# Stick-breaking attention: the scan's products less 1, times differences of neighbouring rows of v, in place of differences of the products times v

## The chip, the core and the metric

The kernel runs on one core of a Trainium2 chip, in float32 throughout. The metric is the device time of one execution in microseconds (us). Work goes to five instruction queues that each run in order: PE (the matrix engine), DVE (vector), ACT (scalar), POOL (GpSimd) and SP, which only issues transfers (DMAs). The order on each engine is fixed when the program is built: a scheduler places the instructions by its own estimates, and the chip doesn't reorder them. An instruction that waits therefore holds up all that is queued behind it on its engine.

## What is computed

One layer of a hybrid decoder for 1024 positions of width 1024: a projection into three groups (short convolution, attention with 8 heads of 64, a spatial gating unit), an output projection, a squared-ReLU MLP and a gated embedding, each with a residual. The change is in the attention. For query t, with z its products with the keys:

```python
log_beta = jax.nn.log_sigmoid(z)
log_rem = jnp.where(causal, jax.nn.log_sigmoid(-z), 0.0)
suffix = lax.cumsum(log_rem, axis=3, reverse=True) - log_rem
weights = jnp.where(causal, jnp.exp(log_beta + suffix), 0.0)
o = jnp.einsum('bhqk,bkhd->bqhd', weights, vj)
```

With r[s] the product of sigmoid(-z) over all causal positions from s on (and 1 past the last), the weight of position s is r[s+1] - r[s]. So o is the sum over s of (r[s+1] - r[s]) v[s]. Summed by parts, the same o is the sum of (r[s] - 1)(v[s-1] - v[s]), with v[-1] = 0: the differences can be taken along the keys of v once per head, in place of along the keys of r for every query.

## The kernel before

Matrix products keep near float32 precision by splitting an operand into a rounded part "hi" (ACT writes it) and the remainder "lo" (mostly DVE, sometimes POOL): the helper `split`, L131 to L139. A product is three matmuls (L161 to L163).

The attention runs in four passes, one for a pair of heads each. `project(pr)` (L345) makes q, k and v of a pair: for each of eight tiles t of 128 positions it runs 24 matmuls of 384 columns into a bank `qkv_ps`, of which there are two. It then reads the bank: squares on ACT (L376), sums on DVE (L379), the power -1/2 on POOL (`rs`, L170), the scaled `qk` on DVE (L384), and v as V hi on ACT and V lo on DVE (L137, L138). Only then is the bank free, so tile t+2 can't start on PE before this chain of tile t has ended. `turn_qk` (L395) then turns q and k and writes QS, KH and KL.

`attend(pr)` (L423) has two generators. `stick` makes, for two query tiles, the products z on PE, the sigmoid on ACT into `rem` (L452), the running product from the right on DVE (`scan`, L457), and then `wt`, the differences of neighbouring columns of `rem` (L464): on DVE for t in (3, 5, 7), on POOL for t in (0, 1, 2, 4, 6), with a memset of the last column on POOL (L463). `gather` turns `wt` on PE (L486) into a bank `w_tr`, splits it into wT_hi and wT_lo (L489), and multiplies by V into `av` (L504). `rem` has 3 buffers and `wt` 4.

`weave` (L269) interleaves the attention of a pair with the projection of the next pair (for the last pair with the convolution) by counted units, so on PE both stand in one queue. The first projection runs without an attention beside it. The results of a head are added by a transfer that POOL issues (`y_both`, L515) and stored by SP (`y_dram`, L435). Between the steps, POOL and ACT issue transfers that add up blocks of later weights in DRAM (`w_sums`, `u_sums`, L305, L308, L322). They are issued behind the last `wt` of POOL and the last sigmoid of ACT (L293, `last_pool`, `last_act`).

SP issues the weights of the coming projections into 7 stage buffers (L67), and the stores, all in one queue. After the attention follow the output projection, the two MLP products and the gate (L814), which take some two thirds of the time.

Of the kernel before, what the change touches and what calls it, by code (L numbers as in the profile page):

```python
# [7 lines left out]
F32 = mybir.dt.float32  # L8
# [6 lines left out]
P = 128  # L15
# [8 lines left out]
STAGES = 7  # L24
WBUFS = 20
SLOTS = 56
LATE = {"w": 22, "raw": 4, "sum": 6, "tmp": 12, "R": 2}
KC = 8
WARM = 8
# [4 lines left out]
def hybrid_block(ctx: ExitStack, tc: tile.TileContext, a: dict):  # L34
# [93 lines left out]

    last_hi, last_power = [None], [None]

    def split(src, hi, lo, scale=None, low=nc.vector):  # L131

        if scale is None:
            last_hi[0] = nc.scalar.copy(hi, src)  # L134
            low.tensor_tensor(out=lo, in0=src, in1=hi, op=ALU.subtract)  # L135
        else:
            nc.scalar.activation(hi, src, AF.Copy, scale=scale)  # L137
            nc.vector.scalar_tensor_tensor(out=lo, in0=src, scalar=scale, in1=hi,  # L138
                                           op0=ALU.mult, op1=ALU.subtract)  # L139
# [199 lines left out]
    last_pool, last_act = [None], [None]  # L339
    summed = []  # L340
    heads = {}
    y_kept = []
# [2 lines left out]
    def project(pr):  # L345
# [11 lines left out]
        for t in range(KT):  # L357
# [24 lines left out]
            if t % 2 == 0:  # L382
# [2 lines left out]
                out=qk[:, t % 2].rearrange("p (h d) -> p h d", d=HD),  # L385
                in0=ps[:, :256].rearrange("p (h d) -> p h d", d=HD),
                in1=rs.unsqueeze(2).broadcast_to([P, 4, HD]), op=ALU.mult)
            if t % 2 == 0:
                V[t // 2] = slot("V", F32R, (P, 2, 2, 2, HD))
            v = V[t // 2][:, t % 2]  # L390
            split(ps[:, 256:].rearrange("p (h d) -> p h d", d=HD), v[:, :, 0], v[:, :, 1], scale=r1[t])
            if t % 2 == 1:
                later(72, lambda t=t, qk=qk: turn_qk(heads[pr], t, qk))

    def turn_qk(head, t, qk):  # L395

# [26 lines left out]
    def attend(pr):  # L423
# [13 lines left out]
        def stick(hh, g):  # L437
            weights[hh, g] = []
            for t in (2 * g, 2 * g + 1):
                W = (t + 1) * P  # L440
                th, ts = block(t)
                rem = at.tile([P, T], F32, tag="rem", name=name("rem"), bufs=3)
                wt = at.tile([P, T], F32, tag="wt", name=name("wt"), bufs=4)
                for kh in reversed(range(th + 1)):
                    n = min(HT, W - kh * HT)
                    ks = slice(kh * HT, kh * HT + n)
                    z = bank(ps_z, "z")[:, :n]
                    nc.tensor.matmul(z, QS[hh][th][:, ts], KH[hh][kh][:, :n],
                                     start=True, stop=False)
                    nc.tensor.matmul(z, QS[hh][th][:, ts], KL[hh][kh][:, :n],  # L450
                                     start=False, stop=True)
                    last_act[0] = nc.scalar.activation(rem[:, ks], z, AF.Sigmoid,  # L452
                                                       scale=-HD ** -0.5)


                back = rem[:, :W][:, ::-1]
                nc.vector.tensor_tensor_scan(out=back, data0=back,  # L457
                                             data1=after[:, T - W:][:, ::-1], initial=1.0,
                                             op0=ALU.mult, op1=ALU.max)


                on_vector = t in (3, 5, 7)
                nc.gpsimd.memset(wt[:, W - 1:W], 0.0)  # L463
                done = (nc.vector if on_vector else nc.gpsimd).tensor_tensor(  # L464
                    out=wt[:, :W - 1], in0=rem[:, 1:W], in1=rem[:, :W - 1], op=ALU.subtract)
                if not on_vector:
                    last_pool[0] = done
                weights[hh, g].append(wt)
                yield 2 * (t + 1) + 8

        def gather(hh, g):
# [5 lines left out]
            def turn(j):  # L477
# [8 lines left out]
                        nc.tensor.transpose(tr[:, n:n + P], wts[i][:, kb * P:(kb + 1) * P], ident)  # L486
# [40 lines left out]
    def attention():  # L527
# [6 lines left out]
        for i, (pr, *step) in enumerate(steps):  # L534
            if i + 1 < len(steps):
                nxt, *ahead = steps[i + 1]
                if nxt not in parts:
                    parts[nxt] = attend(nxt)
                yield from parts[nxt][0](*ahead)
            block_sums(i, (last_pool[0], last_act[0]))  # L540
            if pr == 3:
                up_sums(last_pool[0], last_act[0])
            yield from parts[pr][1](*step)
            if i % 2 == 1:
                parts[pr][2]()
            if i % 8 == 7:
                yield None
# [10 lines left out]
    def gating():  # L558
# [35 lines left out]
        for t in range(KT):  # L594
# [6 lines left out]
                root(th)  # L601
                yield 1
            if t % 4 == 0:
                vp = [at.tile([P, 4, 4 * HD], F32R, tag="rem", name=name("vn"), bufs=3)
                      for _ in range(2)]
                vus = []
            if t % 2 == 0:
                vus.append(at.tile([P, 2, HT], F32, tag="wt", name=name("vu"), bufs=4))
# [74 lines left out]
    for n in range(KT):  # L683
# [1 line left out]
        st = stage(a["w_vu"][n])  # L685
        vu_parts.append(pair("vu"))
        split(st, *vu_parts[n])
        pp = at.tile([P, T], F32, tag="wt", name=name("pp"), bufs=4)
# [368 lines left out]


    g_sums = dram.tile([4, 4, P, HT], F32, name="g_sums")
    pace = const.tile([P, 2], F32, name="pace")  # L1060
    def gate_sums(i, behind):

        if not 0 <= i < 16:
# [281 lines left out]
```

## Time and profile before

| | us |
|---|---|
| three runs | 1208.08, 1208.18, 1209.59 |
| median of the runs | 1208.18 |
| the profiled execution, first to last instruction (span) | 1205.0 |
| attention and its projections, about | 75 to 410 of the span |

The profile gives no time of its own for the profiled execution beside the span. The median run is 3.2 us longer than the span, which lies before the first and after the last instruction. In the tables that follow, "busy" is the time in which an engine executed, and the name behind an arrow is what ended the idle time before an instruction. Busy times of matmuls that follow each other overlap. A row of a timeline begins with the start in us from the span's start and the duration in us.

### The profile page before, as it was taken

The numbers are of one execution on the slowest core, as the hardware profiler recorded it, in microseconds if no ns is written. First come the engines' busy times: TensorE is split into PE (matmuls) and PEld (weight loads), VectorE is DVE, ScalarE is ACT, GpSimd is POOL, SyncE is SP. The second block draws the span as 40 slices with busy tenths as digits, with TensorE's granted clock in tenths as the row PEclk, the third lists the DMA queues.
The fourth block names the chain that finished last, engine by engine and source line by source line (L and its number), as shares of the span: only waits on it lengthen the run. The fifth ranks groups of instructions, "written<-read, shape, count | busy, mean of one in ns | idle before, by whom it ended". The sixth has DMA issues, their size and how long they took to land.

```text
span 1205.0 us, 17538 instructions
## 1 busy us (share of the span) xinstructions
PE 1181.0 (98%) x5788; PEld 1007.1 (84%) x5788; DVE 885.7 (73%) x1310; ACT 595.5 (49%) x1148; POOL 400.5 (33%) x472
## 2 busy tenths in 40 slices
PE   9999899998999999999999999999999999999997
PEld 7899899898888888888888888888888888888886
DVE  7846898989896667868877777787664657753697
ACT  7735565565643466733334333356543444456642
POOL 3324355464352222045354453421023301013412
PEclk9999999999999999999999999999999999999999
DMA  9602359999673776679998989777889975644857
GB/s 311 233 18 90 130 172 262 253 194 167 140 146 95 196 263 204 204 207 261 265 240 249 264 238 260 221 257 277 300 267 295 290 249 175 231 146 119 181 155 209
DMA packets 127963, 254.03 MB, mean 211 GB/s; under 512 B 14496, under 2 KB 22432, under 8 KB 127168
## 3 DMA queue, kind: packets, MB, share of 16 engines
q1 hardware_dynamic: 94992, 168.08, 41.4%
q0 software_dynamic: 27664, 57.05, 25.2%
q10 hardware_dynamic: 5216, 27.79, 6.4%
q8 instruction: 45, 0.74, 0.3%
q14 instruction: 46, 0.38, 0.1%
HBM read 192.30 MB, written 92.80 MB: 237 GB/s over the span
## 4 chain that ended last, share of the span: by engine, by line
PE 88%; DVE 8%; ACT 1%; issue 1%; DMA 1%; POOL 1%; SPq 0%; DVEq 0%; ACTq 0%; POOLq 0%
PE f_ps L814 25%; PE d_ps L814 25%; PE g_ps L814 6%; DVE rem L457 3%; PE qkv_ps L161 3%; PE qkv_ps L162 2%; PE qkv_ps L163 2%; PE o_ps L161 2%; PE o_ps L163 2%; PE o_ps L162 2%; PE av L504 2%; PE cv_ps L163 2%; PE cv_ps L161 2%; PE cv_ps L162 2%; PE w_tr L486 1%; PE vu_ps L162 1%
## 5 line engine op out<-in xcount | busy, mean ns | idle before, releaser
L135 DVE TENSOR_TENSOR w_lo<-raw,w_hi 128x512 fp32r<-128x512 f32 x280 | 243.1, 872 | 85.0 <-ACT w_hi L134 83.1
L134 ACT CAST w_hi<-raw 128x512 fp32r<-128x512 f32 x280 | 172.5, 620 | 240.5 <-PE d_ps L814 115.4
L814 PE MATMUL f_ps<-hn_hi,w_hi 128*128 128x512 f32 x448 | 175.2, 392 | 0.0
L814 PE MATMUL f_ps<-hn_lo,w_hi 128*128 128x512 f32 x448 | 174.9, 390 | 0.0
L814 PE MATMUL d_ps<-f_hi,w_hi 128*128 128x512 f32 x448 | 174.8, 390 | 0.0
L814 PE MATMUL f_ps<-hn_hi,w_lo 128*128 128x512 f32 x448 | 174.6, 391 | 0.0
L814 PE MATMUL d_ps<-f_hi,w_lo 128*128 128x512 f32 x448 | 174.3, 389 | 0.0
L814 PE MATMUL d_ps<-f_lo,w_hi 128*128 128x512 f32 x448 | 174.3, 389 | 0.0
L457 DVE TENSOR_TENSOR_SCAN rem<-rem,after 128x128 f32<-128x128 f32 (+3 forms) x64 | 90.9, 1431 | 13.3 <-ACT rem L452 13.3
L814 PEld LDWEIGHTS f_ps<-hn_lo,w_hi 128*128 128x128 f32 x448 | 84.5, 189 | 17.9 <-issue 0.2
L814 PEld LDWEIGHTS f_ps<-hn_hi,w_hi 128*128 128x128 f32 x448 | 84.5, 189 | 17.8 <-issue 0.2
L814 PEld LDWEIGHTS f_ps<-hn_hi,w_lo 128*128 128x128 f32 x448 | 84.5, 189 | 17.6
L814 PEld LDWEIGHTS d_ps<-f_hi,w_hi 128*128 128x128 f32 x448 | 84.1, 188 | 17.7 <-issue 0.2
L814 PEld LDWEIGHTS d_ps<-f_hi,w_lo 128*128 128x128 f32 x448 | 84.1, 188 | 17.6
L814 PEld LDWEIGHTS d_ps<-f_lo,w_hi 128*128 128x128 f32 x448 | 84.1, 188 | 17.5 <-issue 0.2
L161 PE MATMUL qkv_ps<-whi,xn_hi 128*128 128x384 f32 x256 | 88.8, 347 | 0.9 <-DVE V L138 0.8
L162 PE MATMUL qkv_ps<-wlo,xn_hi 128*128 128x384 f32 x256 | 86.6, 338 | 0.0
L163 PE MATMUL qkv_ps<-whi,xn_lo 128*128 128x384 f32 x256 | 86.3, 337 | 0.0
L135 DVE TENSOR_TENSOR f_lo<-raw,f_hi 128x512 fp32r<-128x512 f32 x112 | 78.2, 728 | 8.5 <-ACT f_hi L134 8.2
L134 ACT CAST f_hi<-raw 128x512 fp32r<-128x512 f32 x112 | 67.1, 620 | 25.6 <-DMA raw<-f_dram 21.6
L800 POOL TENSOR_TENSOR S<-S,sq 128x512 f32<-128x512 f32 x19 | 25.6, 1347 | 160.1 <-ACT sq L876 160.1
L452 ACT ACTIVATE rem<-z 128x128 f32<-128x128 f32 (+3 forms) x96 | 46.7, 500 | 24.3 <-PE z L450 21.6
(250 smaller groups left out, 2618.9 us busy)
## 6 DMA issues: line engine op xcount, KB each, us to landing
raw<-in_w_ff SPq DMA_DIRECT2D x148, 256.0 KB, 4.2
raw<-f_dram SPq DMA_DIRECT2D x112, 256.0 KB, 5.1
raw<-w_sums SPq DMA_DIRECT2D x64, 256.0 KB, 4.1
f_dram<-f SPq DMA_DIRECT2D x48, 256.0 KB, 3.9
f_dram<-t SPq DMA_DIRECT2D x48, 256.0 KB, 4.0
w_sums<-in_w_ff POOLq DMA_DIRECT2D x8, 1024.0 KB, 12.1
w_sums<-w_sums POOLq DMA_DIRECT2D x8, 1024.0 KB, 15.3
raw<-in_w_out SPq DMA_DIRECT2D x28, 256.0 KB, 3.5
```

The lines of the kernel that those rows point to most:

```text
L134: last_hi[0] = nc.scalar.copy(hi, src)
L135: low.tensor_tensor(out=lo, in0=src, in1=hi, op=ALU.subtract)
L161: nc.tensor.matmul(ps, lh, rh, start=first and i == 0, stop=False)
L162: nc.tensor.matmul(ps, lh, rl, start=False, stop=False)
L163: done = nc.tensor.matmul(ps, ll, rh, start=False, stop=last and i == len(terms) - 1)
L452: last_act[0] = nc.scalar.activation(rem[:, ks], z, AF.Sigmoid, scale=-HD ** -0.5)
L457: nc.vector.tensor_tensor_scan(out=back, data0=back, data1=after[:, T - W:][:, ::-1], initial=1.0, op0=ALU.mult, op1=ALU.max)
L486: nc.tensor.transpose(tr[:, n:n + P], wts[i][:, kb * P:(kb + 1) * P], ident)
L504: nc.tensor.matmul(av[:, first * P:], lhs, part[:, o:o + m], start=kb == 0 and part is hi, stop=kb == 2 * g + 1 and part is lo)
L800: return eng.tensor_tensor(out=out, in0=x, in1=y, op=ALU.add)
L814: done = nc.tensor.matmul(bank, l, r, start=first and k == 0 and i == 0, stop=k == len(b) - 1 and i == 2, skip_group_check=True)
```

## The change

1. `stick` no longer makes `wt`: the 64 differences (24 on DVE, 40 on POOL) and the 64 memsets on POOL go. `gather` turns `rem` itself. `rem` now has 6 buffers and serves also the gating unit's and the embedding's tiles that had been in `wt`.
2. The 80 splits of `w_tr` subtract 1 on the way: hi is an ACT activation with a bias of -1, lo is a three-operand instruction of DVE, (w_tr - 1) - hi.
3. v leaves the bank with one ACT instruction a tile into `v_raw`, which holds four tiles; the 32 V lo of DVE go.
4. After four tiles, `v_steps` makes the differences: SP moves `v_raw` down by one row (a transfer from rows 0 to 126 to rows 1 to 127 of `v_step`, one that brings three single rows from row 127, and, for the second half, one single row from the half before; for the first half a memset of one row on POOL), POOL subtracts `v_raw` (one instruction of 128x512), and each half of `v_step` is split: hi by a cast on ACT, lo on POOL. This happens twice for each pair of heads, eight times in all.
5. The transfers that add up weights are now issued behind a small copy on POOL (`pace`, 128x2) from the newest `rem`, 32 in all, since no `wt` is there to be issued behind.

```diff
+REMS = 6
...
-    def split(src, hi, lo, scale=None, low=nc.vector):
-
-        if scale is None:
+    def split(src, hi, lo, scale=None, low=nc.vector, offset=None):
+
+        if offset is not None:
+            nc.scalar.activation(hi, src, AF.Copy, bias=offset)
+            nc.vector.scalar_tensor_tensor(out=lo, in0=src, scalar=offset, in1=hi,
+                                           op0=ALU.add, op1=ALU.subtract)
+        elif scale is None:
...
-            if t % 2 == 0:
-                V[t // 2] = slot("V", F32R, (P, 2, 2, 2, HD))
-            v = V[t // 2][:, t % 2]
-            split(ps[:, 256:].rearrange("p (h d) -> p h d", d=HD), v[:, :, 0], v[:, :, 1], scale=r1[t])
+            if t % 4 == 0:
+                raw_before = raw if t else None
+                raw = at.tile([P, 4, P], F32, tag="v_raw", name=name("v_raw"), bufs=2)
+            nc.scalar.activation(raw[:, t % 4], ps[:, 256:], AF.Copy, scale=r1[t])
             if t % 2 == 1:
                 later(72, lambda t=t, qk=qk: turn_qk(heads[pr], t, qk))
+            if t % 4 == 3:
+                later(24, lambda th=th, v=raw, b=raw_before: v_steps(V, th, v, b))
+
+    def v_steps(V, th, raw, before):
+
+        step = slot("v_step", shape=(P, 4, P))
+        nc.sync.dma_start(step[1:], raw[:P - 1])
+        nc.sync.dma_start(step[:1, 1:], raw[P - 1:, :3])
+        if before is None:
+            nc.gpsimd.memset(step[:1, 0], 0.0)
+        else:
+            nc.sync.dma_start(step[:1, 0], before[P - 1:, 3])
+        nc.gpsimd.tensor_tensor(out=step, in0=step, in1=raw, op=ALU.subtract)
+        for j in range(2):
+            v = V[2 * th + j] = slot("V", F32R, (P, 2, 2, 2, HD))
+            split(step[:, 2 * j:2 * j + 2].rearrange("p t (h d) -> p t h d", d=HD),
+                  v[:, :, :, 0], v[:, :, :, 1], low=nc.gpsimd)
+        return 0
...
-                on_vector = t in (3, 5, 7)
-                nc.gpsimd.memset(wt[:, W - 1:W], 0.0)
-                done = (nc.vector if on_vector else nc.gpsimd).tensor_tensor(
-                    out=wt[:, :W - 1], in0=rem[:, 1:W], in1=rem[:, :W - 1], op=ALU.subtract)
-                if not on_vector:
-                    last_pool[0] = done
-                weights[hh, g].append(wt)
+                last_rem[0] = rem
+                weights[hh, g].append(rem)
...
-                split(tr[:, :n], hi[:, :n], lo[:, :n])
+                split(tr[:, :n], hi[:, :n], lo[:, :n], offset=-1.0)
...
+            last_pool[0] = nc.gpsimd.tensor_copy(pace, last_rem[0][:, :2])
             block_sums(i, (last_pool[0], last_act[0]))
```

The scheduler places the new instructions among the old. Two places matter below.

On POOL, at the end of the first projection, these rows stood before. `rs_1207`, `rs_1244`, `rs_1289` and `rs_1326` are the powers of the tiles 4, 5, 6 and 7, and `rs_1512` that of tile 0 of the second projection; a power is followed by DVE's `qk`, which frees a bank.

```order
L170 TENSOR_TENSOR rs_1207<-ss_1205,mhalf 128x4
L170 TENSOR_TENSOR rs_1244<-ss_1242,mhalf 128x4
L170 TENSOR_TENSOR rs_1289<-ss_1287,mhalf 128x4
L464 TENSOR_TENSOR wt_1348<-rem_1347 128x127
L464 TENSOR_TENSOR wt_1421<-rem_1420 128x255
L135 TENSOR_TENSOR wlo_1371<-stage_1368,whi_1370 128x384
```

At the same place the changed program has these rows. Here `rs_1214`, `rs_1250` and `rs_1294` are the powers of the tiles 4, 5 and 6.

```order
L175 TENSOR_TENSOR rs_1214<-ss_1212,mhalf 128x4
L409 MEMSET v_step_1198 1x128
L412 TENSOR_TENSOR v_step_1198<-v_step_1198,v_raw_993 128x512
L175 TENSOR_TENSOR rs_1250<-ss_1248,mhalf 128x4
L140 TENSOR_TENSOR V_1203<-v_step_1198,V_1203 128x4x64
L140 TENSOR_TENSOR V_1206<-v_step_1198,V_1206 128x4x64
L175 TENSOR_TENSOR rs_1294<-ss_1292,mhalf 128x4
```

Between the powers of tiles 4 and 5 now stands the subtraction that waits for SP's transfer of the first half of v, and two lo of V between those of tiles 5 and 6.

The second half of the same pair is met a little later, at the start of the second projection, where `rs_1508` and `rs_1594` are the powers of its tiles 0 and 1. Again POOL, changed program:

```order
L175 TENSOR_TENSOR rs_1508<-ss_1506,mhalf 128x4
L412 TENSOR_TENSOR v_step_1349<-v_step_1349,v_raw_1218 128x512
L175 TENSOR_TENSOR rs_1594<-ss_1592,mhalf 128x4
L368 MEMSET KL_1414 64x512
L368 MEMSET KL_1416 64x512
L140 TENSOR_TENSOR V_1354<-v_step_1349,V_1354 128x4x64
```

The subtraction again stands directly ahead of a power; before, nothing that waits for a transfer stood there.

On SP the transfers of that second half come after the weights of a coming projection (`stage`) and ahead of the stores of `y_both`:

```order
L68 DMA stage_3003<-in_w_qkv 128x384
L406 DMA v_step_1349<-v_raw_1218 127x512
L407 DMA v_step_1349<-v_raw_1218 1x16x24
L411 DMA v_step_1349<-v_raw_993 1x16x8
L459 DMA y_dram<-y_both_1481 64x512
```

The program carries the single rows as 16 pieces of 24 and of 8 numbers and a store as 64 rows; the big transfer it carries as 127 rows of 512 numbers.

More of the change, by code (lines that the diff above doesn't have):

```diff
@@ L337, in up_sums @@
                            lambda of: w_block("w_ff1", of, i // 4), nc.scalar)
-    last_pool, last_act = [None], [None]
+    last_pool, last_act, last_rem = [None], [None], [None]
+    pace = const.tile([P, 2], F32, name="pace")
     summed = []
@@ L441, in stick @@
                 th, ts = block(t)
-                rem = at.tile([P, T], F32, tag="rem", name=name("rem"), bufs=3)
-                wt = at.tile([P, T], F32, tag="wt", name=name("wt"), bufs=4)
+                rem = at.tile([P, T], F32, tag="rem", name=name("rem"), bufs=REMS)
                 for kh in reversed(range(th + 1)):
@@ L603, in gating @@
             if t % 4 == 0:
-                vp = [at.tile([P, 4, 4 * HD], F32R, tag="rem", name=name("vn"), bufs=3)
+                vp = [at.tile([P, 4, 4 * HD], F32R, tag="rem", name=name("vn"), bufs=REMS)
                       for _ in range(2)]
@@ L607, in gating @@
             if t % 2 == 0:
-                vus.append(at.tile([P, 2, HT], F32, tag="wt", name=name("vu"), bufs=4))
+                vus.append(at.tile([P, 2, HT], F32, tag="rem", name=name("vu"), bufs=REMS))
             vu = vus[-1][:, t % 2]
@@ L687, in hybrid_block @@
         split(st, *vu_parts[n])
-        pp = at.tile([P, T], F32, tag="wt", name=name("pp"), bufs=4)
+        pp = at.tile([P, T], F32, tag="rem", name=name("pp"), bufs=REMS)
         for h in range(2):
@@ L1059, in hybrid_block @@
     g_sums = dram.tile([4, 4, P, HT], F32, name="g_sums")
-    pace = const.tile([P, 2], F32, name="pace")
     def gate_sums(i, behind):
```

## Prediction

> **What bounds the kernel now.** I read the page first: which engine is busy over the span.
>
> ```profile
> PE 1181.0 (98%) x5788; PEld 1007.1 (84%) x5788; DVE 885.7 (73%) x1310; ACT 595.5 (49%) x1148; POOL 400.5 (33%) x472
> ```
>
> PE is the bound, so the change is worth what PE idles where the change acts. The table by windows tells how much (columns: PE, PEld, DVE, ACT, POOL busy us with counts, granted clock, DMA share, GB/s): the whole attention stage, then its densest part.
>
> ```profile
> 100.00:425.00 325.00, 311.68 (x1865) 282.78 (x1864) 273.25 (x404) 175.00 (x411) 150.18 (x199) 1.00 0.70 172
> 150.00:300.00 150.00, 142.18 (x920) 134.08 (x921) 136.75 (x201) 86.83 (x215) 81.36 (x110) 1.00 0.87 209
> ```
>
> PE idles 325 - 311.68 = 13.3 us in the stage, and 7.8 of them in the dense part, where DVE is busy 136.75 of 150 (91%). The clock is granted in full, so it plays no part. The list of PE's waits in 100 to 425 names what PE waited for (columns: total us, times, longest).
>
> ```profile
> PE w_tr L486 <- DVE KL L409: 3.6, 4, 1.5
> PE w_tr L486 <- DVE wt L464: 3.2, 3, 1.6
> PE av L504 <- DVE wT_lo L135: 2.9, 4, 1.8
> PE qk_tr L403 <- DVE qk L384: 1.5, 1, 1.5
> PE qkv_ps L161 <- DVE V L138: 0.8, 2, 0.5
> PE av L504 <- DVE y_b L522: 0.5, 1, 0.5
> PE w_tr L486 <- DVE wT_lo L135: 0.3, 1, 0.3
> ```
>
> All 12.8 us are waits for DVE. The change takes work from DVE, so this sum is the most it can gain.
>
> **What goes and what is added on the engines.** The groups of instructions that go, from the groups by line of the stage (first three rows) and of the time up to 620 us with shapes apart:
>
> ```profile
> L464 DVE TENSOR_TENSOR wt<-rem 128x511 f32<-128x511 f32 (+2 forms) x24 | 26.0, 1083 | 1.2 <-PE w_tr L486 0.8
> L464 POOL TENSOR_TENSOR wt<-rem 128x127 f32<-128x127 f32 (+4 forms) x40 | 43.8, 1111 | 41.7 <-DVE rem L457 41.7
> L463 POOL MEMSET wt<- 128x1 f32 x60 | 11.5, 310 | 41.0 <-PE w_tr L486 40.7
> L138 DVE SCALAR_TENSOR_TENSOR V<-qkv_ps,r,V 128x128 fp32r<-128x128 f32 x32 | 11.0, 345 | 5.1 <-ACT V L137 4.8
> ```
>
> DVE loses 26.0 + 11.0 = 37.0 us. Its 80 lo of w_tr become three-operand instructions; whether these are dearer is read from a pair of 128x512 rows that both read a bank:
>
> ```profile
> L135 DVE TENSOR_TENSOR wT_lo<-w_tr,wT_hi 128x512 fp32r<-128x512 f32 x48 | 32.1, 680 | 3.4 <-ACT wT_hi L134 2.7
> L977 DVE SCALAR_TENSOR_TENSOR f<-f_ps,S 128x512 f32<-128x512 f32 x5 | 3.4, 685 | 1.7 <-PE f_ps L814 1.7
> ```
>
> 5 ns each, 80 x 5 ns = 0.4 us: nothing. On ACT the 32 V hi become 32 evictions of the same size (no cost), the 80 hi with a bias cost what the sigmoid costs more than the cast, and 16 casts of 128x256 come on top.
>
> ```profile
> L452 ACT ACTIVATE rem<-z 128x512 f32<-128x512 f32 x48 | 28.9, 607 | 12.0 <-PE z L450 11.3
> L134 ACT CAST wT_hi<-w_tr 128x512 fp32r<-128x512 f32 x48 | 27.9, 592 | 10.3 <-PE w_tr L486 9.3 <-DVE cv_acc L663 0.6
> L134 ACT CAST vn<-vu 128x256 fp32r<-128x256 f32 x8 | 3.2, 401 | 11.3 <-DVE vu L624 11.3
> ```
>
> 80 x 15 ns + 16 x 401 ns = 7.6 us on an engine that is busy 175 of 325: hidden by its idle time. POOL loses 43.8 + 11.5 = 55.3 us and gets eight 128x512 subtractions, 16 lo of 128x256 (two thirds of a 128x384) and 32 paces.
>
> ```profile
> L800 POOL TENSOR_TENSOR S<-S,sq 128x512 f32<-128x512 f32 x7 | 9.1, 1298 | 41.1 <-ACT sq L876 41.1
> L797 POOL TENSOR_TENSOR t<-t,v 128x512 f32<-128x512 f32 x5 | 9.7, 1936 | 0.0
> L135 POOL TENSOR_TENSOR wlo<-stage,whi 128x384 fp32r<-128x384 f32 x12 | 16.8, 1515 | 1.3 <-ACT whi L134 1.3
> L1065 POOL COPY pace<-h 128x2 f32<-128x2 f32 x12 | 5.6, 469 | 100.4 <-DVE h L800 74.8 <-DVE h L797 25.6
> ```
>
> 8 x 1.6 + 16 x 1.01 + 32 x 0.47 = 44 us, less than goes. The paces wait for a scan as the `wt` did (41.7 us of such waits), so the pacing of the weight sums stays.
>
> **The gain.** The waits for `wt` (3.2) and V (0.8) go with their instructions: 4.0 us. The other 8.8 us are waits for instructions that stood in DVE's queue; with 37 of 273.25 us gone the queue is shorter, and I take two thirds, 6 us. Gain 10; bounds 4.0 and 12.8. The scan now feeds the turning on PE directly, so what is late next is KL and wT_lo, on the same queue.
>
> **The new wait.** V now comes by way of SP, and POOL waits for the transfer. Two prices bound it: what a store of half the size takes to land in this stage (it is carried as 64 rows, which split evenly over 16 DMA engines), and what the 127 rows take if one engine moves them all. The first three rows are of the windows 100 to 150, 250 to 300 and 150 to 200 (the last number is the median landing in us), the fourth is the page's row of the queue that SP's transfers take, the fifth a stretch at the start of the program in which the 16 DMA engines were all busy.
>
> ```profile
> y_dram<-y_both SPq DMA_DIRECT2D x1, 128.0 KB, 2.3
> y_dram<-y_both SPq DMA_DIRECT2D x3, 128.0 KB, 5.5
> stage<-in_w_qkv SPq DMA_DIRECT2D x7, 192.0 KB, 15.0
> q1 hardware_dynamic: 94992, 168.08, 41.4%
> 25.00:32.00 7.00, 7.00 (x33) 5.79 (x32) 6.84 (x12) 6.16 (x12) 1.60 (x3) 1.00 1.04 404
> ```
>
> Cheap end: twice the store's bytes, about 3 us on a quiet and 11 on a busy queue. Dear end: q1's packets took 0.414 x 16 x 1205 / 94992 = 84 ns for 168.08 MB / 94992 = 1769 bytes; 127 x 2048 bytes on one engine are 147 such, 12.3 us. At the 404 / 16 = 25.3 GB/s of an engine in the busy stretch, the 260 KB take 10.3 us. With the some 1.9 us that the store's 2.3 hold beside its four packets an engine that is 12.2 to 14.2 us. Which? Every other transfer that the order shows has 128, 64 or 16 pieces, and the program carries even a single row as 16 pieces; 127 is prime and has no equal parts. So I take the dear end, 14 us on quiet queues, and keep both ends for the range.
>
> The Trainium skill speaks to this, in "DMA: Bandwidth & Descriptors", section "Why a DMA increments its semaphore by 16 and not by 1": a transfer is spread over the largest number up to 16 that divides the slowest dimension of both sides, and 127 partitions go to one engine. No run here shows it yet. By that rule the sum is the slower one below; by the store's row it would be the gain alone. The same page's rate of an engine, 27 GiB/s, would make it an estimated 9 us of moving.
>
> Now who waits. POOL stands at the subtraction, and the powers behind it wait, so DVE's `qk`, so the bank, so PE's tile after next. First transfer, rows of the timeline: V of tile 3, then for tile 5 the power, `qk` and V, then PE's first matmul of tile 7, which needs tile 5's bank.
>
> ```profile
> 98.59 0.37 ACT L137 ACTIVATE V<-qkv_ps,r 128x128 fp32r<-128x128 f32 x1 [1.42 <-DVE qk L384]
> 105.70 1.01 POOL L170 TENSOR_TENSOR rs<-ss,mhalf 128x4 f32<-128x4 f32 x1 [3.62 <-DVE ss L379]
> 106.75 0.42 DVE L384 TENSOR_TENSOR qk<-qkv_ps,rs 128x256 f32<-128x256 f32 x1 [1.12 <-POOL rs L170]
> 107.21 0.37 ACT L137 ACTIVATE V<-qkv_ps,r 128x128 fp32r<-128x128 f32 x1 [1.35 <-DVE qk L384]
> 109.60 0.42 PE L161 MATMUL qkv_ps<-whi,xn_hi 128*128 128x384 f32 x1
> ```
>
> Issue at 99.0, landing at 111.2 to 113.2, subtraction to 112.8 to 114.8, power 1.0, `qk` and eviction 0.9: the bank is free at 114.7 to 116.7 in place of 107.6, and PE, due at 109.6, waits 5.1 to 7.1 us. I take 5.5. With the cheap end the subtraction ends at 104 and nobody waits.
>
> Second transfer: V of tile 7, the power of tile 1 of the next projection, and PE's tile 3.
>
> ```profile
> 121.74 0.37 ACT L137 ACTIVATE V<-qkv_ps,r 128x128 fp32r<-128x128 f32 x1 [3.83 <-DVE qk L384]
> 128.21 1.01 POOL L170 TENSOR_TENSOR rs<-ss,mhalf 128x4 f32<-128x4 f32 x1 [3.05 <-DVE ss L379]
> 133.53 0.33 PE L161 MATMUL qkv_ps<-whi,xn_hi 128*128 128x384 f32 x1
> ```
>
> All shifted by 5.5, and the 3.83 before V gone: issue at 124, landing 138, subtraction to 139.6, power, `qk` and eviction to 141.5, while PE is due at 139: 2.5, or up to 7 if V isn't earlier; I take 4.5. Of the other six, the third and the eighth cost nothing: in POOL's order the third stands behind weights and a weight sum, the eighth behind the last power. The four others stand ahead of a power, in windows whose DMA share is 0.87 on average, where one engine is shared and V can be late for `av` too. Nothing in the trace shows their meeting; bounds 0 and 10 each (a landing of 24 in place of 14), and I take 3.5, below the first two, since PE then has attention work between the tiles. Together 5.5 + 4.5 + 14 = 24 us.
>
> **Smaller edits.** Six shared buffers for `rem` stand for three and four: two steps in hand and one ahead, as the four of `wt` allowed, no cost. SP's queue behind the transfers holds weights fetched a projection ahead and stores that PE doesn't wait for: no cost unless a store is late for a `KL` slot, which is in the range.
>
> **Sum.** 1205.0 - 10 + 24 = 1219.0 for the span; with the 3.2 us that the median has more than the span, 1222.
>
> **Rivals.** (1) Faster: the transfer is spread over the engines and lands in 3 to 11 us. For it speaks the store's 2.3 us; against it the 127. The point at which it decides is a landing by 104 for the first transfer, 5 us after the issue. Then only the gain of 4 to 12.8 is left, most likely 10: 1198 (1195 to 1204). (2) No change: the transfer is slow, but only the first two are met by PE, since in the later projections attention work fills the time; 10 lost, 10 gained: 1208 (1206 to 1210). For it speaks that in the later projections PE has the turning, z and `av` of a pair between the tiles, against it DVE's 91% there, which leaves the chain behind a late power little room. (3) Slower still: in the dense part the one engine is shared with the weight sums as the 15.0 us of seven loads of 192 KB show, and four landings of 24 us and more cost 10 each: 10 + 40 - 10, 1248.
>
> **How the numbers follow.** About 0.2%, 2.4 us, is what a measurement of this kernel can tell. Forecast, slower by 3 to 34 us: 0.62, its own range 1211 to 1242. Rival 1: 0.18. Rival 2: 0.11, of which 0.02 falls to faster. Rival 3: 0.09. Faster 0.20, same 0.09, slower 0.71. The range from 1197 to 1242 leaves out rival 3 and the lower end of rival 1, some 0.13; the two ends of the landing's price make it that wide.
>
> **What would show it.** The issue-to-landing time of `v_step`: 12 us and more right, under 6 wrong. A wait of POOL at its subtraction, and of PE's `qkv_ps` for `qk` or the eviction near 110 and 139. The waits for `wt` and V gone, and DVE's busy time 37 us less. If PE idles less than 13.3 us in the stage, the prediction is wrong; if V lands late and PE still doesn't wait, the mistake is in who is queued behind it.

## The result and the profile after

The changed kernel takes 1307.25 us (median of 4 runs, 1304.77 to 1308.12) against 1208.13 us before: a ratio of 1.0813, with a 95% interval from 1.0798 to 1.0828. It is slower by 99 us. The prediction said 1222 us with a range to 1242: the direction was right, the size was not.

The profiled execution spans 1303.0 us against 1205.0. It took 1304.77 us, 1.8 us more than its span; the 3.2 us that the prediction added to the span also hold some spread between executions, which changes nothing here. The row of busy times from the page after:

```profile
PE 1196.0 (92%) x5788; PEld 1023.2 (79%) x5788; DVE 858.1 (66%) x1254; ACT 598.9 (46%) x1164; POOL 392.2 (30%) x428
```

PE idles 1303 - 1196 = 107 us, where it idled 24 before, and is busy 15 us more for the same 5788 matmuls. These two, 83 and 15, are the 98 us. The table by windows puts the idle time where the change acts (columns as in the prediction; the third figure from the end is the granted clock):

```profile
100.00:425.00 325.00, 234.09 (x1391) 221.41 (x1389) 174.79 (x264) 140.69 (x348) 108.07 (x127) 0.84 0.54 136
```

From 100 to 425 PE is busy 234.09 us where it was busy 311.68, and DVE, which had been the engine to wait for, 174.79. The clock, 1.00 before, is 0.84. PE's waits from 100 to 500 us name new releasers:

```profile
PE qkv_ps L166 <- ACT v_raw L397: 39.7, 3, 19.6
PE av L520 <- ACT wT_hi L135: 29.2, 2, 17.4
PE z L471 <- ACT rem L475: 15.3, 2, 15.0
PE qk_tr L427 <- DVE qk L390: 5.8, 1, 5.8
```

The waits for `wt` and for V are gone, as forecast. Of the four rows that took their place only the last, 5.8 us, is the chain that the prediction followed. The other 84 us are waits for ACT. What ACT waits for stands in the list of all waits, same stretch up to 520:

```profile
POOL v_step L412 <- DMA v_step<-v_raw: 116.1, 7, 22.3
ACT V L139 <- POOL v_step L412: 56.5, 5, 18.9
ACT v_raw L397 <- DMA v_step<-v_raw: 41.3, 3, 20.5
```

So one slow transfer is met by three instructions: POOL's subtraction, ACT's cast to V hi behind it, and ACT's eviction into `v_raw`. The timeline shows each case once. The first transfer, issued at 99.67, goes as the prediction had it, by POOL, the power and `qk` to PE. (PE's queue has the turning of `qk` ahead of the tile that waits for the bank, so it stops there; the bank's last reader, ACT's eviction, ends at 116.46, and the tile's first matmul starts at 116.51.)

```profile
113.37 1.26 POOL L412 TENSOR_TENSOR v_step<-v_step,v_raw 128x512 f32<-128x512 f32 x1 [10.46 <-DMA v_step<-v_raw]
115.63 0.42 DVE L390 TENSOR_TENSOR qk<-qkv_ps,rs 128x256 f32<-128x256 f32 x1 [9.32 <-POOL rs L175]
116.11 0.69 PE L427 MATMUL qk_tr<-ident,qk 128*128 128x128 f32 x2 [5.81 <-DVE qk L390]
```

The second, issued at 128.68, reaches PE by ACT's eviction of the next projection's first tile:

```profile
144.05 0.37 ACT L397 ACTIVATE v_raw<-qkv_ps,r 128x128 f32<-128x128 f32 x1 [10.15 <-DMA v_step<-v_raw]
144.47 0.69 PE L166 MATMUL qkv_ps<-whi,xn_hi 128*128 128x384 f32 x1 [10.01 <-ACT v_raw L397]
```

The fifth, issued at 250.86, reaches PE by the cast: ACT stands at it for 18.87 us, and the next cast of the turned weights, for which PE waits, is queued behind it.

```profile
282.67 0.40 ACT L139 CAST V<-v_step 128x256 fp32r<-128x256 f32 x1 [18.87 <-POOL v_step L412]
283.92 0.58 PE L520 MATMUL av<-wT_hi,V 128*128 128x256 f32 x1 [17.37 <-ACT wT_hi L135]
```

During this wait the clock falls to half, and it is still there when PE works again (windows of 4, 4 and 8 us from 284 on):

```profile
284.00:288.00 4.00, 4.00 (x16) 4.00 (x17) 4.00 (x6) 2.48 (x7) 1.35 (x3) 0.50 1.28 459
288.00:292.00 4.00, 4.00 (x25) 3.90 (x24) 2.15 (x5) 2.61 (x9) 1.31 (x2) 0.76 0.07 18
292.00:300.00 8.00, 8.00 (x58) 7.91 (x58) 7.91 (x14) 5.99 (x16) 6.51 (x7) 1.00 0.54 118
```

The 0.76 is a mean: in windows of half a microsecond the clock stands at 0.50 until about 289.9 and at 1.00 from there, so 6 us of work at half lose 3 us. Behind the seven waits of 5.8 us and more of this execution the half clock lasts 2.8 to 6.2 us of work, together 31.6, which loses some 16 us, about what PE's busy time grew.

### The profile page after: what moved, and what is told of

Same layout as the page of the kernel before. It is cut to its first block, busy times and chain, and to the rows that moved or that the text cites. A ratio compares the mean times of both kernels' runs of the same rounds, so it can differ in the third digit from the quotient of the medians.

```text
span 1303.0 us, 17464 instructions
## 1 busy us (share of the span) xinstructions
PE 1196.0 (92%) x5788; PEld 1023.2 (79%) x5788; DVE 858.1 (66%) x1254; ACT 598.9 (46%) x1164; POOL 392.2 (30%) x428
## 4 chain that ended last, share of the span: by engine, by line
PE 75%; DMA 13%; SPq 3%; DVE 3%; POOL 2%; issue 2%; ACT 1%; POOLq 0%; DVEq 0%; ACTq 0%
PE f_ps L831 23%; PE d_ps L831 23%; DMA v_step<-v_raw 8%; PE g_ps L831 6%; SPq L407 3%; DMA y_both<-y_both 2%; PE o_ps L168 2%; PE o_ps L166 2%; PE o_ps L167 2%; PE qkv_ps L166 2%; PE av L520 1%; PE qkv_ps L167 1%; PE qkv_ps L168 1%; DMA stage<-in_w_qkv 1%; PE w_tr L502 1%
## 5 line engine op out<-in xcount | busy, mean ns | idle before, releaser
L140 DVE TENSOR_TENSOR w_lo<-raw,w_hi 128x512 fp32r<-128x512 f32 x280 | 257.0, 922 | 90.8 <-ACT w_hi L139 88.8
L480 DVE TENSOR_TENSOR_SCAN rem<-rem,after 128x128 f32<-128x128 f32 (+3 forms) x64 | 88.2, 1388 | 73.2 <-ACT rem L475 73.0
L166 PE MATMUL qkv_ps<-whi,xn_hi 128*128 128x384 f32 x256 | 93.6, 365 | 39.7 <-ACT v_raw L397 39.7
L831 PEld LDWEIGHTS d_ps<-f_hi,w_lo 128*128 128x128 f32 x448 | 84.1, 188 | 17.3
L167 PE MATMUL qkv_ps<-wlo,xn_hi 128*128 128x384 f32 x256 | 91.4, 357 | 0.0
L168 PE MATMUL qkv_ps<-whi,xn_lo 128*128 128x384 f32 x256 | 90.8, 355 | 0.0
L136 DVE SCALAR_TENSOR_TENSOR wT_lo<-w_tr,wT_hi 128x512 fp32r<-128x512 f32 (+1 forms) x80 | 49.0, 628 | 60.6 <-ACT wT_hi L135 60.0
L166 PEld LDWEIGHTS qkv_ps<-whi,xn_hi 128*128 128x128 f32 x256 | 51.6, 202 | 41.3 <-ACT v_raw L397 40.6
```

What stands on the lines that cost most here:

```text
L136: nc.vector.scalar_tensor_tensor(out=lo, in0=src, scalar=offset, in1=hi, op0=ALU.add, op1=ALU.subtract)
L166: nc.tensor.matmul(ps, lh, rh, start=first and i == 0, stop=False)
L167: nc.tensor.matmul(ps, lh, rl, start=False, stop=False)
L168: done = nc.tensor.matmul(ps, ll, rh, start=False, stop=last and i == len(terms) - 1)
L480: nc.vector.tensor_tensor_scan(out=back, data0=back, data1=after[:, T - W:][:, ::-1], initial=1.0, op0=ALU.mult, op1=ALU.max)
L831: done = nc.tensor.matmul(bank, l, r, start=first and k == 0 and i == 0, stop=k == len(b) - 1 and i == 2, skip_group_check=True)
```

## The experiments

**The gain alone.** `v_steps` without its transfers (and without the memset of the first row, which the cut code holds too):

```diff
-        nc.sync.dma_start(step[1:], raw[:P - 1])
...
-        nc.gpsimd.tensor_tensor(out=step, in0=step, in1=raw, op=ALU.subtract)
+        nc.gpsimd.tensor_tensor(out=step, in0=raw, in1=raw, op=ALU.subtract)
```

> The transfers of v_steps are left out, and POOL subtracts v_raw from itself, so that V is zero: the attention's result is left out, the rest of the work is as in the changed kernel. Theory (all of the loss comes from the transfers and what waits for them, and the rest of the change is the gain that was forecast): 1198 us (1194 to 1204). Rival (the detour by POOL, the splits with -1 or the paces cost something of their own): 1208 or more.

Measured 1199.16 us, ratio 0.9921 (0.9903 to 0.9940). All other work of the change is in it, and it is 10 us faster than before. So the whole loss, 108 us from here, comes with the transfers: from what waits for them, and from the order that the scheduler makes with them in the program. (It places all instructions anew for each edit; in this run the order differs from the changed kernel's on every engine. The same holds for all runs below but the four cuts among each other.) The rival is out. The row of its page:

```profile
PE 1177.6 (98%) x5788; PEld 1008.4 (84%) x5788; DVE 851.7 (71%) x1254; ACT 597.0 (50%) x1164; POOL 384.1 (32%) x424
```

**How many engines.** Four kernels cut the 127 rows in two at different places. By their traces they have the same order of work on every engine, so among the four only the cut differs.

```diff
-        nc.sync.dma_start(step[1:], raw[:P - 1])
+        nc.sync.dma_start(step[1:113], raw[:112])
+        nc.sync.dma_start(step[113:], raw[112:P - 1])
```

112 and 15 rows:

> The 127 rows go as two transfers, 112 rows and 15 rows, both from SP; nothing else is edited. Theory (the whole loss comes from one DMA engine carrying 127 rows, and is paid by ACT, which stands at the buffer of v_raw and at the cast of V, and by PE behind it): both land within 3 to 6 us, PE's waits for v_raw (39.7 us), wT_hi (29.2) and the sigmoid (15.3) go, the granted clock is 0.99 again, and the time is 1198 us (1194 to 1204), below the kernel before. Rival (the other edits cost the time: the splits with -1, the paces, the shared buffers, the detour of V as such): the landing is short all the same, and the time stays above 1250.

113 and 14:

> Two transfers again, but 113 rows (a prime number) and 14 rows, so that the order of all engines is that of the spread kernel and only the cut differs by one row. Theory: the 113 rows go by one engine and land after 11 to 21 us, and the time is 1280 to 1310. Rival (the spread kernel differs by the order that its second transfer brings, not by the engines): the time is that of the spread kernel within 5 us.

122 and 5:

> 122 rows (2 x 61) and 5 rows, order as in the spread kernel. Theory (the largest count up to 16 that divides the rows is the number of engines, so two here): landing about half, 6 to 11 us. Each of PE's waits of 5.8, 10.0, 10.0, 17.4, 19.6, 11.8 and 15.0 us becomes some 7 to 9 us shorter, 30 us of them are left, less the gain: 1230 us (1215 to 1245). Rival (any number that 16 doesn't divide goes by one engine): as the 113 rows, above 1280.

124 and 3:

> 124 rows (4 x 31) and 3 rows, order as in the spread kernel. Theory: four engines, landing 4 to 7 us, all of PE's waits but some 10 us gone: 1206 us (1198 to 1215). Rival (one engine whenever 16 doesn't divide): above 1280. Rival (what counts is only whether the landing is below the 5 us of my first estimate): as the spread kernel within 3 us.

| rows of the larger piece | by the rule: engines, rows on each | median us | ratio to before (95%) | PE idle us |
|---|---|---|---|---|
| 112 | 16, 7 | 1234.81 | 1.0195 (1.0164 to 1.0227) | 43 |
| 124 | 4, 31 | 1259.09 | 1.0413 (1.0385 to 1.0441) | 63 |
| 122 | 2, 61 | 1282.99 | 1.0611 (1.0583 to 1.0639) | 91 (in an execution of 1290.78) |
| 113 | 1, 113 | 1320.76 | 1.0929 (1.0902 to 1.0956) | 122 |

One row more, 113 in place of 112, costs 86 us. What the first transfer moves is seen in the GB/s row of the DMA view, 99 to 112 us in 40 slices, when hardly anything else is in flight. In order: the changed kernel (127 rows), then 122, 124 and 112.

```profile
GB/s 0 0 0 0 0 0 19 6 23 13 19 6 19 0 25 25 25 25 25 32 25 25 25 25 25 25 25 25 25 25 25 25 25 25 25 25 25 25 25 25
```
```profile
GB/s 0 0 0 0 0 0 32 19 38 38 19 38 13 44 50 44 57 64 54 50 50 57 50 50 38 0 0 0 0 0 0 0 0 0 0 0 0 0 0 0
```
```profile
GB/s 0 0 38 50 32 13 32 76 69 65 89 101 101 64 50 26 0 0 0 0 0 0 0 0 0 0 0 0 0 0 0 0 0 0 0 0 0 0 0 0
```
```profile
GB/s 0 0 0 0 0 221 265 208 107 0 5 0 0 0 0 0 0 0 0 0 0 0 0 0 0 0 0 0 0 0 0 0 0 0 0 0 0 0 0 0
```

25, 50, 100 and over 200 GB/s: one, two, four and many engines of 25. (The 113 rows, not shown, move at 25 as well.) The rivals that put every number that 16 doesn't divide on one engine, or the effect on the order, are out, and so is the one that had 124 rows within 3 us of 112. In time each row more on the slowest engine costs 0.7 to 1.0 us: 24 us for the 24 rows from 7 to 31, 24 for the next 30, 38 for the next 52. Between these four no threshold shows below which the landing is free. All four are above the times I expected, the spread one by 37 us: it lands fast and is still slower than before. Something besides the engine is left in it.

**What is left in the spread kernel.** Its SP rows and ACT's row of the fourth transfer say what. The last tile of that half was evicted by 194.19.

```profile
208.13 0.49 SPq L460 DMA_DIRECT2D y_dram<-y_both  x1
208.72 0.54 SPq L406 DMA_DIRECT2D v_step<-v_raw  x1
```
```profile
218.44 0.37 ACT L397 ACTIVATE v_raw<-qkv_ps,r 128x128 f32<-128x128 f32 x1 [14.99 <-DMA v_step<-v_raw]
```

The issue is 14.5 us late. Ahead of it in SP's queue stands a store of `y_both`, which waits for the sum of two halves that POOL's transfer makes. SP's own list of waits shows that SP stood like this before the change as well, when no transfer of v was behind it (first row before, second in the spread kernel):

```profile
SPq L435 <- DMA y_both<-y_both: 159.6, 12, 35.7
```
```profile
SPq L460 <- DMA y_both<-y_both: 147.7, 11, 31.1
```

Two runs take away one end each. Issue by ACT (`nc.scalar` in place of `nc.sync` in `v_steps`):

> The spread cut (112 and 15 rows), and all transfers of v_steps are issued by ACT, which writes v_raw, in place of SP. Theory (what is left of the loss in the spread kernel is SP's queue: up to 14.5 us between the eviction and the issue, since SP stands at stores that wait for the sums of y_both and at stage buffers): issue within 2 us of the last eviction, PE's 20.7 us of waits for v_raw under 5, time 1205 us (1198 to 1212). Rival (what is left is the landing of 6 us median itself and the detour by POOL): the waits of PE stay above 12 us and the time above 1222.

More buffers for `v_raw`: three in place of two, although the expectation says four (and six stage buffers, not seven, so this run is not free of a second edit):

> The spread cut from SP, with four buffers of v_raw in place of two (and six stage buffers in place of seven, for the room). Theory (PE's waits of 20.7 us in the spread kernel are ACT standing at a buffer that a transfer, issued late by SP, still has to read): those waits go although SP's issues stay late, time 1214 us (1206 to 1222). Rival (the late issue reaches PE by POOL and V instead): the time stays above 1228.

Measured 1221.34 (ratio 1.0094, 1.0078 to 1.0110) and 1221.90 (1.0105, 1.0089 to 1.0119). Each takes 13 us away, and PE's wait for `v_raw` falls from 20.7 us to 1.1 and 6.2. That fits a late issue and a held buffer as the two ends of one chain; a run with both edits, which would show it, is missing. Neither reaches the time I expected of it (1205, 1214). With ACT as the issuer, PE's longest wait is now 7.4 us for a cast of KH, ahead of which ACT idles 6.63 us among its issues.

**One instruction that stands, taken away, with the 127 rows kept.** First the cast of V hi, moved to POOL:

```diff
-            split(step[:, 2 * j:2 * j + 2]..., v[:, :, :, 0], v[:, :, :, 1], low=nc.gpsimd)
+            nc.gpsimd.tensor_copy(v[:, :, :, 0], src)
+            nc.gpsimd.tensor_tensor(out=v[:, :, :, 1], in0=src, in1=v[:, :, :, 0], op=ALU.subtract)
```

> The transfer of 127 rows stays as in the changed kernel; only the cast of V hi is moved from ACT to POOL, which makes V lo anyway. Theory (ACT's order carries the late V to PE: the cast stands 56.5 us for the subtraction and holds the casts of wT_hi and the sigmoids behind it, which belong to the pair before and don't need this V): PE's waits for wT_hi (29.2) and the sigmoid (15.3) fall below 15 together, and the time is 1265 us (1250 to 1285). Rival (V itself is late for the products that need it): PE waits for V in av instead, and the time stays at 1295 to 1312.

Then the wait for the buffer. The last reader of the older `v_raw` is the single row of 0.5 KB, issued behind the 127 rows; here it goes first:

```diff
+            nc.sync.dma_start(step[:1, 0], before[P - 1:, 3])
         nc.sync.dma_start(step[1:], raw[:P - 1])
         nc.sync.dma_start(step[:1, 1:], raw[P - 1:, :3])
-            nc.sync.dma_start(step[:1, 0], before[P - 1:, 3])
```

> One edit on the changed kernel: the single row that comes from the half before (0.5 KB) is issued ahead of the 127 rows in place of behind them. Theory (ACT stands at v_raw for this one row: it is the last reader of the older of the two buffers, and is queued behind the 127 rows): ACT's 41.3 us of waits for v_raw fall below 5 and PE's 39.7 with them; part comes back as PE's wait behind POOL's subtraction and power, as in the kernel with the cast on POOL, so the time is 1290 us (1278 to 1302). Rival (the buffer is held by the 127 rows that read it themselves): the waits for v_raw stay, time 1303 to 1312.

Measured 1299.37 (ratio 1.0744, 1.0727 to 1.0760) and 1305.35 (1.0792, 1.0772 to 1.0812): 8 and 2 us, nearly nothing. Both times lie where the rivals put them, but not for the rivals' reasons: PE waits only 2.5 us for V, and ACT's wait for `v_raw` does fall, from 41.3 to 8.2. But PE's waits have changed places. With the cast on POOL, up to 520 us:

```profile
PE qkv_ps L166 <- ACT v_raw L397: 64.1, 5, 20.7
PE qk_tr L429 <- DVE qk L390: 15.2, 2, 9.4
```

With the row first:

```profile
PE av L520 <- ACT wT_hi L135: 30.1, 2, 17.4
PE av L520 <- ACT y_both L529: 28.2, 4, 12.3
PE z L471 <- ACT rem L475: 15.7, 3, 15.2
PE qkv_ps L166 <- ACT v_raw L397: 9.2, 3, 6.1
```

In the first the waits for `wT_hi` and the sigmoid, 44.5 us, are down to 2.4, as the theory said; in their place POOL now stands longer and its power is late (DVE's `qk` waits 56.0 us for it, 21.6 before this edit). In the second ACT's eviction hardly stands for the transfer any more, and ACT stands for the same landing at the cast (105.1 us in place of 56.5). So my theory of ACT alone fell: the three instructions are parallel ways from one landing to PE, and closing one leaves the others. The 0.5 KB row was for the most part what held the buffer.

**The sums queued later.** If what counts is what is queued behind the waiting instruction, the cure is to queue it later. The subtraction is now emitted after the power of a tile one to two tiles on, and kept behind it:

```diff
+        late_steps.append([3 - th, steps])
...
             power_mhalf(rs, ss, 4)
+            for w in late_steps:
+                w[0] -= 1
+            while late_steps and late_steps[0][0] <= 0:
+                with tc.issue_after(last_power[0].ins):
+                    late_steps.pop(0)[1]()
```

With the 127 rows in one piece, from SP:

> The 127 rows still go in one piece; the single row goes first, and the subtraction with what follows is queued on POOL behind the power of a tile that is one to two tiles later (the last half, which has no projection behind it, is left). Theory (a slow landing costs only what stands in a queue behind the instruction that waits for it): POOL's 116.1 us of waits at the subtraction fall below 50, PE idles some 30 us in place of 107, and the time is 1222 us (1205 to 1240). Rival (the transfer costs by itself, through SP being held, late weights and stores): above 1260.

112 and 15 rows, from SP:

> As the kernel before it, with the 127 rows cut into 112 and 15. Theory (short landing, and nobody stands at what is left of it): 1203 us (1197 to 1211), at or below the kernel before. Rival (SP's late issues, up to 14.5 us, still reach PE through V): 1215 or more.

112 and 15 rows, from ACT:

> As the kernel before it, with all transfers of v_steps issued by ACT. Theory (no late issue, short landing, nobody stands): 1202 us (1197 to 1209). Rival (the four issues take 2 us each of ACT's queue, as the 6.6 us ahead of a cast of KH with PE's wait of 7.4 behind it showed): 1212 or more, above the kernel that issues from SP.

127 rows, from ACT, the small ones first:

> The 127 rows go in one piece, on one engine, with the later sums, and all transfers of v_steps are issued by ACT, the two small ones ahead of the 127 rows. Theory (a slow landing costs what stands behind it, and where the sums are queued later and no issue is late, nothing much stands): POOL's waits at the subtraction below 50 us, time 1225 us (1212 to 1242). Rival (the one engine costs by itself, whoever issues it: the queue that issues is held, and other transfers of that engine are late): 1260 or more.

| rows, issued by | median us | ratio to before (95%) |
|---|---|---|
| 127, SP | 1291.27 | 1.0679 (1.0663 to 1.0696) |
| 127, ACT | 1273.94 | 1.0524 (1.0510 to 1.0538) |
| 112 and 15, SP | 1218.64 | 1.0080 (1.0064 to 1.0095) |
| 112 and 15, ACT | 1211.79 | 1.0022 (1.0012 to 1.0032) |

With 127 rows from SP the first transfer does what the theory says: the subtraction starts at 112.91, about as before, but POOL waits 1.54 us for it in place of 10.46, and PE's 5.81 us are gone. The others don't: POOL's waits at the subtraction are 106.8 us in all, not below 50, and PE idles 90 us, not 30. The third shows the rival's way. Behind its issue at 183.62 SP needs 22.52 us to issue seven loads of weights, ACT stands for one of them, and PE behind ACT:

```profile
187.49 22.52 SPq L68 DMA_DIRECT2D stage<-in_w_qkv  x7
```
```profile
208.17 0.51 ACT L139 CAST whi<-stage 128x384 fp32r<-128x384 f32 x1 [22.96 <-DMA stage<-in_w_qkv]
```
```profile
210.31 0.58 PE L533 MATMUL av<-wT_hi,V 128*128 128x256 f32 x1 [21.04 <-ACT y_both L542]
```

These 21 us are not the weights' alone. POOL stood 23.41 us for the same transfer, until 207.98; its subtraction ends at 209.25, and the cast of V hi, next in ACT's queue, could not start before that. So my 1222 was wrong for this run: the later place doesn't outlast a landing of 24 us, and on SP the loads of weights behind the one engine are late besides. The run from ACT leaves SP free (and has the three single rows go first too) and takes 17 us off; it stays in its rival's range, 1260 or more, with 67.0 us of POOL's waits where I expected less than 50. Its subtractions of the fifth to the eighth transfer, and PE's waits behind the sixth and the eighth:

```profile
274.49 1.29 POOL L420 TENSOR_TENSOR v_step<-v_step,v_raw 128x512 f32<-128x512 f32 x1 [4.24 <-PE qkv_ps L168]
318.65 1.25 POOL L420 TENSOR_TENSOR v_step<-v_step,v_raw 128x512 f32<-128x512 f32 x1 [22.41 <-DMA v_step<-v_raw]
360.73 1.27 POOL L420 TENSOR_TENSOR v_step<-v_step,v_raw 128x512 f32<-128x512 f32 x1 [4.88 <-DMA v_step<-v_raw]
396.78 1.26 POOL L420 TENSOR_TENSOR v_step<-v_step,v_raw 128x512 f32<-128x512 f32 x1 [17.01 <-DMA v_step<-v_raw]
```
```profile
321.19 0.69 PE L484 MATMUL z<-KH,QS 128*128 128x384 f32 x1 [16.31 <-ACT rem L488]
399.32 0.80 PE L484 MATMUL z<-KH,QS 128*128 128x512 f32 x1 [17.28 <-ACT rem L488]
```

The fifth and the seventh belong to first halves, where the sum stands later: PE waits at most 1.4 us behind them. The sixth and the eighth are second halves with less or no delay, and PE waits 16 and 17 us. (The sixth was issued at 290.48 and is met at 318.65: 28 us, where the first of the changed kernel, on quiet queues, was met 13.7 us after its issue.) So where the sum is queued far enough back, the landing costs PE little, and elsewhere what is left of it. Both theories hold in part: one part of the price is what stands behind the landing, another the queue that issues (from ACT the next issue behind the 127 rows took 5.87 us once); how large each is, these runs don't separate. With the split cut from ACT both are nearly gone, 1211.79 us, though 10 us above what I expected; its rival (slower than the run from SP) is wrong too. From SP the split cut takes 1218.64, 7 us more, in its rival's range (1215 or more).

**A version below the kernel before.** The best run had one standing cast left, in the last half. There V hi goes to POOL:

```diff
+                if th and 3 in heads and V is heads[3][3]:
+                    nc.gpsimd.tensor_copy(v[:, :, :, 0], src)
```

> The kernel with the 112 and 15 rows issued by ACT and the later sums, and in the last half, where no later power stands, V hi made by POOL in place of ACT. Theory (PE's wait of 4.2 us for a sigmoid at 334 is ACT standing at that cast): that wait goes, time 1208 us (1204 to 1211), level with the kernel before. Rival (the products of the last half need V then anyway): unchanged at 1211 to 1213.

Measured 1206.53 us, ratio 0.9965 (0.9952 to 0.9978): below the kernel before by 0.35%, and 101 us below the changed one. PE's longest waits up to 520 us are now:

```profile
PE av L539 <- ACT y_both L548: 6.0, 1, 6.0
PE w_tr L521 <- DVE KL L452: 1.5, 1, 1.5
```

The wait of 4.2 us for the sigmoid is gone. The 6.0 stand behind a row of ACT that idles 6.80 us around its issues of the small transfers; whether that is the issue being held was not tried. About 7 us are left to the kernel without the transfers.

## Why the prediction was wrong

The step that failed is the price of the four transfers in the later projections, 3.5 us each: they cost 10.0 to 19.6, by waits of ACT that the prediction didn't follow. Term by term:

- **The gain** (10 us, bounds 4.0 and 12.8): right in size, partly by luck. Without the transfers the kernel is 10.1 us faster. But in its profile PE's waits from 95 to 520 fall only from 12.8 to 7.3 us, 4.7 of these new, for the sigmoid; the rest of the gain is 3.4 us less of PE's busy time, which the sum didn't have. The three-operand splits cost nothing, as said: wT_lo of 128x512 takes 680 ns before and after.
- **DVE 37 us less**: 27.6 less. Busy times of other DVE groups grew: the 280 `w_lo` of 128x512, splits of later weights, take 257.0 us in place of 243.1, and each of the 23 `wlo` of 128x384 in the first 620 us takes 1001 ns in place of 905. It had no effect on the end.
- **One engine, 12.2 to 14.2 us on a quiet queue**: right. The 127 rows, issued at 99.67, had landed when the subtraction began at 113.37, and the single rows issued behind them took 12.7 us; they moved at 25 GB/s. The rule of the Trainium skill ("DMA: Bandwidth & Descriptors", section "Why a DMA increments its semaphore by 16 and not by 1") was weighed there with 127 rows; the cuts at 112, 113, 122 and 124 rows bear it out, and by the rate of that page the estimate of the moving alone had been 9 us, where the packets of the 127 rows took 11.5.
- **First transfer 5.5 us**: 5.8, by the chain that was followed.
- **Second transfer 4.5 us**: 10.0, by another chain, ACT at `v_raw`.
- **Third and eighth nothing**: the third yes. The eighth cost 15.0: behind POOL's subtraction no power stood, as said, but ACT's cast stood for it and held a sigmoid.
- **Four others 3.5 us each, "bounds 0 and 10 each"**: 10.0, 17.4, 19.6 and 11.8 us, 59 in place of 14. This is the step that failed, the paragraph "Now who waits". It followed the landing through POOL's queue alone, and asked for ACT only whether its added casts find idle time ("hidden by its idle time"). The question to ask of ACT was which of its new instructions wait for the transfer, and what is queued behind them. Two do: the cast to V hi, and the first eviction of the half after, whose buffer has two copies and is read by the single row behind the 127 rows. The upper bound of 10 failed with it: it counted only what a landing of 24 us has over one of 14, as if other work always covered the first 14, and ACT's order left hardly any cover. The landings were longer as well: from the issue of the 127 rows to the subtraction that waited for them these four took 20.5 to 30.5 us.
- **"The clock is granted in full, so it plays no part"**: it was so before and not after. Each long wait is followed by 2.8 to 6.2 us of work at 0.50; PE's busy time grew by 15 us.
- **The rivals.** The slower one (1248) had the right mechanism in the landings, 20 to 30 us in the dense part, and the right sign; its price of 10 us for each was too low for the same reason. The spread did not happen, and the second rival, PE having other work between the tiles, was the opposite of what happened in the later projections.
- **SP's queue**: "no cost unless a store is late". The reverse cost: stores held the transfers. In the spread kernel, issuing from ACT instead takes 13 us off.

Summed in the prediction's own terms: 5.8 + 10.0 + 58.8 + 15.0 = 90 us of PE's waits in place of 24, and 15 us of clock in place of none. Less the gain of 10, that is 95 of the 98 us.

What stays open: the run with 113 and 14 rows is 13.5 us slower than the one with 127 in one piece although less lies on one engine. A second transfer also moves the order on all engines (SP's issues are later in it), and no run separates the two.

## What to carry to other kernels

When an operand is sent on a detour by a transfer, list every instruction that waits for its landing, on every engine, the readers that hold the source buffer among them, and for each what is queued behind it; each of them is a way to the bound engine of its own, and the price is that of the longest, not of the one that is easiest to follow. Cut a transfer so that its row count splits over the engines before anything else is tuned (112 and 15 rows in place of 127 took 72 us of 99 off here, and one row fewer, 112 in place of 113 in the same order, 86), issue it from a queue in which nothing slow stands ahead, and put its consumer far back in its engine's order. A bound engine that is made to idle also pays afterwards in clock.

## What the runs showed of the hardware

A queue that issues can itself be held behind a transfer that lies on one engine. The issue of the three single rows right behind the 127 (row of the tile `v_step` after; min, median and max in ns):

```profile
L407 SPq DMA_DIRECT2D v_step<-v_raw x8: 562/11038/20422, 100.5 to 403.7; - x8
```

It takes 11 us in the median and up to 20.4, and what SP has queued behind it waits as long. Only the first took 0.56. The four cuts, which have one order, say when: the issue of the small piece right behind the larger one takes 11.4 us in the median and up to 17.3 behind 113 rows, but at most 1.4 behind 122, 0.75 behind 124 and 0.93 behind 112. So SP is held behind 113 or 127 rows on one engine, and not behind 61 on each of two. Whether the single engine or the number of rows on it decides was not tried. The hold may be part of the 38 us that the step from 61 to 113 rows costs.

The rate of one engine, 25 GB/s, shows with 127 and 113 rows, and twice and four times that with 122 and 124, when little else moves. Beside other transfers the 127 rows land later: the subtractions that waited for them in the changed kernel began 13.7 to 30.5 us after their issue.

In the seven long waits of the changed kernel the granted clock falls to 0.50 1.8 to 4.7 us after PE's last matmul, and comes back to 1.00 after 2.8 to 6.2 us of work. The Trainium skill ("TensorE: Matmul & The Clock Gate", section "Part 1: The HAM clock gate (the "warmup" mystery)") says that the half clock is the resting state and that about 3.4 us of sustained work release it; the trace agrees on the half clock, and its 2.8 to 6.2 us lie on both sides of that figure.
